# A hybrid SSM and attention decoder step on one core: SSM loads moved to ScalarE's queue, and probabilities scaled on VectorE

## The chip, the core and the metric

The kernel runs on one core of a Trainium2 chip. The core has five engines with a queue of instructions each: TensorE (PE, matrix products), VectorE (DVE), ScalarE (ACT), GpSimd (POOL) and SyncE (SP, used here for transfers only). The metric is the device time of one execution in microseconds. Three executions of the kernel before took 1873.18, 1874.78 and 1879.98 us; their median is 1874.78.

## The reference, cut to what matters

One layer of a decoder for 256 prompt positions and 8 x 4 sample positions, width 2048: a half-weighted SwiGLU block, a mixer, and a second SwiGLU block. All is float32. The mixer:

```python
z = rmsnorm(x) @ w_in                      # columns: u (1024), q (1024), k (256), v (256)
# SSM group: 64 groups of 16 channels, 64 complex states each
bu = einsum('blgc,gpc->blgp', u, B_bar)
h  = associative_scan(a = lam_bar, bu)      # h[t] = lam_bar * h[t-1] + bu[t]
y  = Re(einsum('blgp,gcp->blgc', h, C)) + D * u
y  = gelu(y);  y = y * sigmoid(y @ w_glu)   # 16x16 per group
# attention group: window 128, 16 query heads on 4 key heads, per-head sink
p  = exp(logits - m);  p = p / (p.sum() + exp(sink - m));  o = p @ v
x  = x + w_out @ concat(rmsnorm(y), rmsnorm(o))
```

The final SSM states, keys and values are outputs too.

## The kernel before

**Tokens and products.** All 288 tokens stand side by side as columns, 4 phases of 72 (8 sample columns and 64 chunks of 4 prompt positions). A float32 product is made as three: weight and activation are split into a high and a low part (`wh`, `wl`, `xh`, `xl`), and `mm3` (L286) issues high x high, low x high and high x low. One weight piece of 128 x 1024 feeds 24 such products of 288 columns.

**Slots.** The order of the whole kernel is written out by hand in class `Weights`. Each call of `next` (L138) is one slot: it splits the piece that is needed two slots later (a cast on ScalarE, L124, into one of 3 buffers, and a subtraction on VectorE, L125), issues the load of the piece six slots ahead on SP's queue (L116, 6 buffers), runs the functions that were put down for this slot (`at`, `spread`), and returns the piece, with which the caller issues its 24 products. So the small products of a slot stand ahead of its 24, and everything that a slot puts on an engine's queue is done in the order of the list. `spread` runs a generator up to its next `yield` in each slot; with `last=True` it starts behind all else in its slot.

**The mixer** begins at slot `base` = 304: 20 projections of two slots each (one key block, eight SSM blocks j = 0 to 7, one key block, two value blocks, eight query blocks), then 32 slots of the output projection. SSM block j is projected in slots base + 2j + 2 and + 3. Its further steps hang on s = base + 2j + 5:

- `ssm_u_store` (L760, slot s): the projected block goes to DRAM, on ScalarE's queue.
- `ssm_u_load` (L763, slot s + 2): four transfers bring it back with positions on other partitions, as tile `U`, on SP's queue.
- `ssm_load_a`, `ssm_load_r`, `ssm_load_b` (L769, L773, L787): tables `ma`, `rot` and `mb` of this block, written to DRAM during the first SwiGLU block, on SP's queue. `ma` and `mb` have two buffers each, `rot` three.
- `ssm_state` (L791, from slot s + 4): 32 small products of `ma` and `U` (L798, the state products), a rotation on VectorE, the scan (L814), a slot later the rotation back (L820 on POOL, L821) into `cs`, a slot later two corrections (L823, L824) and the copy of the final state on ScalarE (L825).
- `ssm_out` (L827, slot s + 9): 48 small products (L833, the output products) and a Gelu on ScalarE.
- `ssm_y_store`, `ssm_y_load` (L839, L845) for two blocks together: to DRAM in four transfers on ScalarE's queue, and back on SP's.
- `ssm_glu` (L853): one product (L856), Tanh, and `y_split`, which makes the high and low parts and adds the squares for the norm. `ssm_norm` (L898) turns the sum into a factor.

`put` is ScalarE's queue for transfers and `get` is SP's (L697).

**Attention.** For a pair of heads i: `q_square`, `sums` (L1017: row sums on TensorE; `row_rsqrt`, twelve small steps on POOL), `scores` (L1035: products, eviction on ScalarE with the factor from `row_rsqrt` (L1049), distance term on VectorE), `softmax` (L980: maximum on VectorE, Exp on ScalarE, sum and reciprocal on VectorE, the scaling on POOL, L1001), `probs_t` (L1056: transposes on TensorE, L1062) and `pv`. `sample` (L1089) does the same for the sample positions. All PSUM results go through eight tiles of one name (`main`), used in turn.

Of the kernel before, what the change touches and what calls it, by code (L numbers as in the profile page):

```python
# [14 lines left out]
ALU = mybir.AluOpType  # L15
AX = mybir.AxisListType

P = 128
# [15 lines left out]
EPS = 1e-6  # L34
# [656 lines left out]
def mix(tc, nc, io, es, W, base, e):  # L691
    act, dve, pool_e, pe = nc.scalar, nc.vector, nc.gpsimd, nc.tensor
    tt, ts, stt = dve.tensor_tensor, dve.tensor_scalar, dve.scalar_tensor_tensor
    x, R, gains, ident, acc = e["x"], e["R"], e["gains"], e["ident"], e["acc"]
    tp, dr, pm, pa = (e[k] for k in ("tp", "dr", "pm", "pa"))
    proj, mm3 = e["proj"], e["mm3"]
    put, get = act.dma_start, nc.sync.dma_start  # L697
# [7 lines left out]
    def aux():  # L705
        return pa.tile([P, 512], F32, name="main")
# [7 lines left out]
    R_ssm = mp.tile([P, N], F32, name="R_ssm")  # L714
# [7 lines left out]
    yd = [dr.tile([2 * P, N], F32, name="yd%d" % j) for j in range(4)]  # L722
# [8 lines left out]
    def y_split(pool, src, g, first, eng=pool_e):  # L731
        hh = pool.tile([P, N], F32R, name="hh", bufs=8)
        if first:
            pool.tile([P, 32], F32, name="gap_y", bufs=1)
        hl = pool.tile([P, N], F32R, name="hl", bufs=8)
        gc = gains[:, g:g + 1]
        act.activation(halved(hh), evens(src), AF.Copy, scale=gc)
        YH.append(hh)
        YL.append(hl)
        sq = tp.tile([P, N], F32, name="sq", bufs=3)  # L740
        act.activation(sq, src, AF.Square)
        yield
        stt(halved(hl), evens(src), gc, halved(hh.bitcast(F32)), op0=ALU.mult, op1=ALU.subtract)  # L743
        if first:
            eng.tensor_copy(acc, sq)
        else:
            eng.tensor_tensor(acc, acc, sq, op=ALU.add)


    MA, MB, ROT, D0, U, CS, UE, YG, YN, GL = ({} for _ in range(10))  # L750
    c4 = [P, 4, NCH]

    def flat(ap):
        return ap.rearrange("p q k -> p (q k)")
# [8 lines left out]
    def ssm_u_load(j):  # L763
        U[j] = sm.tile([P, 4, W1], F32, name="U", bufs=4)
        src = ud[j].rearrange("(q c) (j t) -> j c q t", q=4, j=T)
        for jr in range(T):
            get(U[j][32 * jr:32 * jr + 32], src[jr])

    def ssm_load_a(j):  # L769
        MA[j] = sa.tile([P, 2, 4, P], F32, name="ma", bufs=2)  # L770
# [20 lines left out]
    def ssm_state(j):  # L791
        ma, u, rot = MA.pop(j), U[j], ROT.pop(j)
        b = []
        for i in range(2):
            ps = aux()
            for q in range(4):
                for hh in HALVES:
                    pe.matmul(ps[hh, q * W1:(q + 1) * W1], ma[:, i, q, hh], u[:, q], start=True, stop=True)  # L798
            b.append(ps[:, :N].rearrange("p (q t) -> p q t", q=4))
        br, bi = b[0][:, :, NB:], b[1][:, :, NB:]  # L800
        co, si = rot[:, :, 0, :], rot[:, :, 1, :]
        z, w = (sa.tile([P, 2, 4, NCH], F32, name="r" + n, bufs=2) for n in "zw")
        q = slice(4 * j, 4 * j + 4)
        tt(z[:, 1], br, co, op=ALU.mult)
        tt(w[:, 1], bi, si, op=ALU.mult)
        tt(z[:, 0], bi, co, op=ALU.mult)
        tt(w[:, 0], br, si, op=ALU.mult)
        yield
        for i in range(2):
            tt(fin_s[:, i, q, :], b[i][:, :, :NB], fin_s[:, i, q, :], op=ALU.add)  # L810
        tt(z[:, 1], z[:, 1], w[:, 1], op=ALU.add)
        tt(z[:, 0], z[:, 0], w[:, 0], op=ALU.subtract)
        for i in range(2):
            dve.tensor_tensor_scan(flat(w[:, i]), flat(D0[j % 2]), flat(z[:, i]), 0.0, op0=ALU.mult, op1=ALU.add)  # L814
        yield
        cs = CS[j % 2]
        for i in range(2):
            act.copy(cs[:, i, :, :NB], e["h0"][:, 1 - i, q, :])
        both = [P, 2, 4, NCH]
        pool_e.tensor_tensor(z, w, si[:, None].to_broadcast(both), op=ALU.mult)  # L820
        tt(cs[:, :, :, NB + 1:], w, co[:, None].to_broadcast(both), op=ALU.mult)  # L821
        yield
        tt(cs[:, 1, :, NB + 1:], cs[:, 1, :, NB + 1:], z[:, 0], op=ALU.subtract)  # L823
        tt(cs[:, 0, :, NB + 1:], cs[:, 0, :, NB + 1:], z[:, 1], op=ALU.add)  # L824
        act.copy(fin[:, :, q], cs[:, :, :, W1])  # L825

    def ssm_out(j):  # L827
# [16 lines left out]

    def ssm_y_load(j):  # L845
        YN[j] = sm.tile([P, 2, N], F32, name="yn", bufs=2)
        get(YN[j], yd[j].rearrange("(a p) n -> p a n", a=2))

    def glu_load():
        GL[0] = sm.tile([P, 8, P], F32, name="gl")  # L850
# [2 lines left out]
    def ssm_glu(j):  # L853
        yn = YN[j // 2][:, j % 2]
        ps = aux()
        pe.matmul(ps[:, :N], GL[0][:, j], yn, start=True, stop=True)  # L856
        t = tp.tile([P, N], F32, name="s1")
        act.activation(t, ps[:, :N], AF.Tanh, scale=0.5)
        yield
        y2 = tp.tile([P, N], F32, name="s2")  # L860
        stt(y2, t, 1.0, yn, op0=ALU.add, op1=ALU.mult)
        yield
        yield from y_split(ys, y2, 48 + j, j == 0, dve if j == 7 else pool_e)
# [16 lines left out]
    for j in range(8):  # L880
        s = base + 2 * j + 5
        W.at(s, ssm_u_store, j)
        W.at(s + 1 if j > 1 else base + 1 + j, ssm_load_a, j)
        W.at(s + 1 if j > 1 else base + 2 + j, ssm_load_r, j)
        W.at(s + 2, ssm_u_load, j)
        W.at(s + 2, ssm_decay, j)
        W.spread(s + 4, ssm_state(j), True)
        W.at(s + 6, ssm_load_b, j)
        W.at(s + 9, ssm_out, j)
        if j % 2:  # L890
            W.at(s + 10, ssm_y_store, j // 2)
            W.at(s + 11, ssm_y_load, j // 2)
            W.spread(s + 13, ssm_glu(j - 1))
            W.spread(s + 14, ssm_glu(j))
    W.at(s + 8, state_done)
    W.at(s + 17, ssm_done)

    def ssm_norm():  # L898
        for n, _ in enumerate(e["norm"](e["ones"], acc, R_ssm, 1.0 / 1024, 4 * EPS)):
            if n % 2:  # L900
                yield

    W.spread(s + 19, ssm_norm())

    def tok(ap, blk):

# [73 lines left out]
    def softmax(lg, parts, sink, w):  # L980

        m = mp.tile([P, w], F32, name="sm_m", bufs=4)
        es_ = mp.tile([P, w], F32, name="sm_e", bufs=4)
        l = mp.tile([P, w], F32, name="sm_l", bufs=4)
        for a, (lo, hi) in enumerate(parts):
            dve.tensor_reduce(m[:, 2 * a:2 * a + 2], lg[:, :, lo:hi], axis=AX.X, op=ALU.max)
        tt(m, m, sink, op=ALU.max)
        tt(es_, sink, m, op=ALU.subtract)
        ts(m, m, -1.0, None, op0=ALU.mult)
        yield  # L990
        for a, (lo, hi) in enumerate(parts):
            for hb in range(2):
                c = 2 * a + hb
                act.activation(lg[:, hb, lo:hi], lg[:, hb, lo:hi], AF.Exp, bias=m[:, c:c + 1],  # L994
                               accum_out=l[:, c:c + 1])
        act.activation(es_, es_, AF.Exp)
        yield
        tt(l, l, es_, op=ALU.add)
        dve.reciprocal(l, l)
        for a, (lo, hi) in enumerate(parts):  # L1000
            pool_e.tensor_tensor(lg[:, :, lo:hi], lg[:, :, lo:hi],  # L1001
                                 l[:, 2 * a:2 * a + 2, None].to_broadcast([P, 2, hi - lo]), op=ALU.mult)

    def q_square(i):
        qb = QN[i]
# [29 lines left out]
    def scores(i):  # L1035
        p, g = divmod(i, 4)
        qb, sq = QN.pop(i)
        rq = RQ[i // 2][:, 4 * (i % 2):4 * (i % 2) + 4]
        pss = [aux() for _ in range(2)]
        for a, (bq, bk) in enumerate(((0, 0), (1, 0), (1, 1))):  # L1040
            for hb in range(2):
                pp = slice(64 * hb, 64 * hb + 64)
                pe.matmul(pss[hb][:, 128 * a:128 * a + 128], qb[pp, 128 * bq:128 * bq + 128],
                          tok(kG[pp, p], bk), start=True, stop=True)
        yield
        lg = L[i] = late["a"].tile([P, 2, 384], F32, name="lg", bufs=3)
        for hb in range(2):
            for blk, (lo, hi) in enumerate(((0, 128), (128, 384))):
                act.activation(lg[:, hb, lo:hi], pss[hb][:, lo:hi], AF.Copy,  # L1049
                               scale=rq[:, 2 * blk + hb:2 * blk + hb + 1])  # L1050
        yield
        for hb in range(2):
            stt(lg[:, hb], dist, -SLOPES[heads_of(i)[hb]], lg[:, hb], op0=ALU.mult, op1=ALU.add)
        yield from softmax(lg, ((0, 128), (128, 384)), sinkp[:, 4 * i:4 * i + 4], 4)
# [105 lines left out]
    for p in range(2):  # L1160
        s = base + 2 * (12 + 4 * p + 3) + 2
# [3 lines left out]
    for i in range(8):  # L1165
        p, g = divmod(i, 4)
# [186 lines left out]
```

## Time and profile before

| | before |
|---|---|
| median of 3 executions | 1874.78 us |
| profiled execution | 1878.1 us, span of its instructions 1876.2 us |
| TensorE clock granted, mean | 0.996 |
| VectorE, ScalarE, POOL busy | 64%, 45%, 14% of the span |
| DMA | 359.08 MB moved, 191 GB/s over the span |
| two SwiGLU blocks and w_in, w_out: large products | 14400 of 288 columns |

In the profile, "idle before, releaser" names what ended a wait by the semaphores seen in the trace; where the engine named had long been done, it was another, often a transfer. PEld is the weight load of TensorE, which runs beside its products. A "q" behind an engine's name (SPq, ACTq) is its queue of instructions, with the issue of transfers. The chain that ended last gives TensorE 93% of the span. In a list of transfers the last number is the median time from issue to landing.

### The profile page before, as it was taken

Reading aid. Unit: us, or ns where it says so; the run is one execution under the profiler, and the core shown is the slowest. Engines: PE = TensorE matmul, PEld = TensorE weight load, DVE = VectorE, ACT = ScalarE, POOL = GpSimd, SP = SyncE. Lnnn points to the kernel's source line nnn. Section 1 sums busy time; section 2 is a strip of 40 time slices with the busy share of each in tenths; the row PEclk is TensorE's granted clock in tenths of the full one; section 3 lists DMA queues with packets and bytes.
Section 4 is the critical chain, followed back from the end, with each engine's and each line's share of the span. In section 5 each row is a group of like instructions: output and inputs, shape, how many; then the busy total and the mean of one; then the engine's idle time right before and its main releaser. Section 6 shows DMA issues by size and latency. Waiting matters only on the chain.

```text
span 1876.2 us, 38183 instructions
## 1 busy us (share of the span) xinstructions
PE 1857.0 (99%) x15620; PEld 1839.1 (98%) x15620; DVE 1207.7 (64%) x1857; ACT 853.6 (45%) x1347; POOL 269.0 (14%) x342
## 2 busy tenths in 40 slices
PE   9999999999999999999989999999999999999999
PEld 9999999999999999998988999999999999999999
DVE  6677667666667755688887885555555555555554
ACT  6443444444444444643566554433444334434433
POOL 3201011000100100212236640000000000000000
PEclk9999999999999999999999999999999999999999
DMA  7555656556655764788733455556555565556555
GB/s 277 197 181 163 219 181 214 190 166 230 212 192 162 232 213 147 238 293 292 232 120 135 157 176 185 179 161 188 187 179 168 174 196 180 163 169 207 180 161 160
DMA packets 122624, 359.08 MB, mean 191 GB/s; under 512 B 22064, under 2 KB 30256, under 8 KB 121264
## 3 DMA queue, kind: packets, MB, share of 16 engines
q1 hardware_dynamic: 114496, 340.48, 56.7%
q10 hardware_dynamic: 7952, 16.16, 2.5%
q8 instruction: 122, 2.00, 0.4%
q14 instruction: 54, 0.44, 0.1%
HBM read 338.40 MB, written 20.22 MB: 191 GB/s over the span
## 4 chain that ended last, share of the span: by engine, by line
PE 93%; DVE 3%; ACT 1%; DMA 1%; POOL 1%; issue 1%; SPq 0%; ACTq 0%; POOLq 0%; DVEq 0%
PE main L290 30%; PE main L292 30%; PE main L291 30%; DVE wl L125 1%; ACT wh L124 1%; PE main L833 1%; DMA ud<-t 0%; PE main L798 0%; PE main L623 0%; PE main L629 0%; ACT lg L994 0%; DMA ma<-mats 0%; DMA raw<-in_w_gu 0%; POOL x L1178 0%; POOL lg L1001 0%
## 5 line engine op out<-in xcount | busy, mean ns | idle before, releaser
L125 DVE TENSOR_TENSOR wl<-raw,wh 128x1024 fp32r<-128x1024 f32 (+2 forms) x677 | 754.1, 1114 | 445.0 <-ACT wh L124 443.1
L290 PE MATMUL main<-xh,wh 128*128 128x288 f32 x3136 | 904.9, 289 | 0.5 <-ACT xh L216 0.5
L292 PE MATMUL main<-xh,wl 128*128 128x288 f32 x3136 | 899.7, 287 | 0.7 <-DVE wl L125 0.6
L291 PE MATMUL main<-xl,wh 128*128 128x288 f32 x3136 | 899.4, 287 | 0.1
L124 ACT CAST wh<-raw 128x1024 fp32r<-128x1024 f32 (+2 forms) x677 | 637.9, 944 | 495.9 <-PE main L291 335.4
L290 PEld LDWEIGHTS main<-xh,wh 128*128 128x128 f32 x3136 | 594.6, 190 | 3.9 <-ACT xh L216 0.8
L292 PEld LDWEIGHTS main<-xh,wl 128*128 128x128 f32 x3136 | 594.5, 190 | 1.7 <-DVE wl L125 0.8
L291 PEld LDWEIGHTS main<-xl,wh 128*128 128x128 f32 x3136 | 594.7, 190 | 1.3 <-DVE xl L217 0.8
L290 PE MATMUL main<-hh,wh 128*128 128x288 f32 x1664 | 478.2, 287 | 0.3 <-ACT s L1079 0.3
L291 PE MATMUL main<-hl,wh 128*128 128x288 f32 x1664 | 476.3, 286 | 0.6 <-DVE hl L743 0.6
L292 PE MATMUL main<-hh,wl 128*128 128x288 f32 x1664 | 476.2, 286 | 0.0
L290 PEld LDWEIGHTS main<-hh,wh 128*128 128x128 f32 x1664 | 314.8, 189 | 1.2 <-ACT s L1079 0.8
L291 PEld LDWEIGHTS main<-hl,wh 128*128 128x128 f32 x1664 | 314.8, 189 | 1.0 <-DVE hl L743 0.8
L292 PEld LDWEIGHTS main<-hh,wl 128*128 128x128 f32 x1664 | 314.8, 189 | 0.2 <-DVE wl L125 0.2
L364 POOL TENSOR_TENSOR s<-s,R 128x288 f32<-128x288 f32 x88 | 70.6, 803 | 1139.5 <-ACT s L363 1139.5
L373 ACT CAST hh<-h 128x288 fp32r<-128x288 f32 x88 | 38.1, 433 | 222.5 <-DVE h L372 222.5
L363 ACT ACTIVATE s<-t 128x288 f32<-128x288 f32 x88 | 39.1, 445 | 219.5 <-DVE t L362 219.5
L394 DVE SCALAR_TENSOR_TENSOR x<-main,x 128x288 f32<-128x288 f32 x128 | 58.4, 457 | 39.7 <-PE main L292 39.3
L372 DVE TENSOR_TENSOR h<-main,s 128x288 f32<-128x288 f32 x88 | 40.1, 456 | 55.5 <-PE main L292 55.2
L362 DVE TENSOR_TENSOR t<-main,R 128x288 f32<-128x288 f32 x88 | 40.2, 456 | 44.9 <-PE main L292 44.6
L374 DVE TENSOR_TENSOR hl<-h,hh 128x288 fp32r<-128x288 f32 x88 | 40.4, 459 | 44.0 <-ACT hh L373 44.0
L226 POOL TENSOR_TENSOR acc<-acc,sq 128x288 f32<-128x288 f32 x45 | 45.3, 1006 | 46.0 <-ACT sq L222 45.1
(262 smaller groups left out, 835.8 us busy)
## 6 DMA issues: line engine op xcount, KB each, us to landing
raw<-in_w_gu SPq DMA_DIRECT2D x349, 512.0 KB, 4.1
raw<-in_w_dn SPq DMA_DIRECT2D x128, 384.0 KB, 3.2
raw<-in_w_dn SPq DMA_DIRECT2D x128, 320.0 KB, 3.2
raw<-in_w_in SPq DMA_DIRECT2D x40, 512.0 KB, 4.9
raw<-in_w_out SPq DMA_DIRECT2D x32, 512.0 KB, 3.5
mats<-stage ACTq DMA_DIRECT2D x8, 1536.0 KB, 7.1
mb<-mats SPq DMA_DIRECT2D x8, 768.0 KB, 8.2
ma<-mats SPq DMA_DIRECT2D x8, 512.0 KB, 5.4
```

The lines of the kernel that those rows point to most:

```text
L124: self.nc.scalar.copy(wh[:, :n], t[:, :n])
L125: self.nc.vector.tensor_tensor(wl[:, :n], t[:, :n], wh[:, :n].bitcast(F32), op=ALU.subtract)
L226: eng.tensor_tensor(acc, acc, sq, op=ALU.add)
L290: pe.matmul(ps, wh[:, s], woven(rh[k]), start=first and a == 0, stop=False)
L291: pe.matmul(ps, wh[:, s], woven(rl[k]), start=False, stop=False)
L292: pe.matmul(ps, wl[:, s], woven(rh[k]), start=False, stop=last and a == n - 1)
L362: dve.tensor_tensor(t1, pg[:, :N], R, op=ALU.mult)
L363: act.activation(s1, t1, AF.Silu)
L364: pool_e.tensor_tensor(s2, s1, R, op=ALU.mult)
L372: dve.tensor_tensor(halved(h), evens(pu[:, :N]), evens(s2), op=ALU.mult)
L374: dve.tensor_tensor(hl, h, hh.bitcast(F32), op=ALU.subtract)
L394: dve.scalar_tensor_tensor(x[d], ps[:, :N], 0.5, x[d], op0=ALU.mult, op1=ALU.add)
```

## The change

The loads of `U` and of the SSM results go to ScalarE's queue. `U` is loaded one slot earlier; for j > 1 the tables `ma` and `rot` are loaded one slot earlier and the state products start one slot earlier and so fall into the slot of the output products of block j - 3. The copy of the final state runs one slot later. The second GLU block of a pair runs in the slot of the first. The norm of the SSM group starts one slot earlier and takes one step a slot. In `softmax`, the scaling moves from POOL (one instruction for two heads) to VectorE (one for each head, `ts` is `tensor_scalar`).

```diff
     def ssm_u_load(j):
...
         for jr in range(T):
-            get(U[j][32 * jr:32 * jr + 32], src[jr])
+            put(U[j][32 * jr:32 * jr + 32], src[jr])
...
         tt(cs[:, 0, :, NB + 1:], cs[:, 0, :, NB + 1:], z[:, 1], op=ALU.add)
+        yield
         act.copy(fin[:, :, q], cs[:, :, :, W1])
...
     def ssm_y_load(j):
         YN[j] = sm.tile([P, 2, N], F32, name="yn", bufs=2)
-        get(YN[j], yd[j].rearrange("(a p) n -> p a n", a=2))
+        put(YN[j], yd[j].rearrange("(a p) n -> p a n", a=2))
...
         W.at(s, ssm_u_store, j)
-        W.at(s + 1 if j > 1 else base + 1 + j, ssm_load_a, j)
-        W.at(s + 1 if j > 1 else base + 2 + j, ssm_load_r, j)
-        W.at(s + 2, ssm_u_load, j)
+        W.at(s + 1, ssm_u_load, j)
+        W.at(s if j > 1 else base + 1 + j, ssm_load_a, j)
+        W.at(s if j > 1 else base + 2 + j, ssm_load_r, j)
         W.at(s + 2, ssm_decay, j)
-        W.spread(s + 4, ssm_state(j), True)
+        W.spread(s + (3 if j > 1 else 4), ssm_state(j), True)
...
             W.spread(s + 13, ssm_glu(j - 1))
-            W.spread(s + 14, ssm_glu(j))
+            W.spread(s + 13, ssm_glu(j))
...
-    def ssm_norm():
-        for n, _ in enumerate(e["norm"](e["ones"], acc, R_ssm, 1.0 / 1024, 4 * EPS)):
-            if n % 2:
-                yield
-
-    W.spread(s + 19, ssm_norm())
+    W.spread(s + 18, e["norm"](e["ones"], acc, R_ssm, 1.0 / 1024, 4 * EPS))
...
         for a, (lo, hi) in enumerate(parts):
-            pool_e.tensor_tensor(lg[:, :, lo:hi], lg[:, :, lo:hi],
-                                 l[:, 2 * a:2 * a + 2, None].to_broadcast([P, 2, hi - lo]), op=ALU.mult)
+            for hb in range(2):
+                ts(lg[:, hb, lo:hi], lg[:, hb, lo:hi], l[:, 2 * a + hb:2 * a + hb + 1], None, op0=ALU.mult)
```

## The prediction, made before the result was known

> **What bounds the kernel now.** I read the page, then the waits of TensorE in the stretch of the mixer, then that stretch by windows, then the queues and engines around each wait.
>
> ```profile
> span 1876.2 us, 38183 instructions
> ...
> PE 1857.0 (99%) x15620; PEld 1839.1 (98%) x15620; DVE 1207.7 (64%) x1857; ACT 853.6 (45%) x1347; POOL 269.0 (14%) x342
> ```
>
> TensorE has work 99% of the time, so only its gaps and its slow stretches can be won. By stage:
>
> ```profile
> 843.40:900.00 56.60, 50.58 (x685) 47.50 (x685) 49.32 (x96) 22.08 (x47) 12.26 (x7) 0.97 0.82 271
> ...
> 940.00:1031.00 91.00, 84.86 (x808) 77.26 (x806) 71.32 (x151) 64.16 (x187) 48.18 (x74) 0.94 0.37 124
> ```
>
> The columns are the window, PE, PEld, DVE, ACT and POOL busy, granted clock, DMA share and GB/s. PE lacks 6.0 us in the SSM stage (843 to 900) and 6.1 in the attention stage (940 to 1031), and both run below full clock. The waits of PE in these two stretches:
>
> ```profile
> PE main L798 <- DMA U<-ud: 2.7, 1, 2.7
> PE main L798 <- ACT cs L818: 2.0, 1, 2.0
> PE main L798 <- DVE rw L814: 1.4, 1, 1.4
> ```
>
> ```profile
> PE main L1062 <- POOL lg L1001: 3.7, 3, 2.2
> PE main L1025 <- ACT qsq L1007: 2.1, 1, 2.1
> ```
>
> The state products (L798) wait three times, 6.1 us. Only the first is named as the load of U; in the others the engine named had long been done and the last U loads were still under way, so I count all three as late U. The transposes (L1062) wait for the scaling on POOL, and the sums (L1025) once.
>
> ```profile
> 873.00:876.40 3.40, 1.44 (x36) 1.25 (x34) 3.37 (x5) 1.78 (x4) 1.86 (x1) 1.00 0.74 213
> 876.40:879.80 3.40, 3.40 (x20) 3.26 (x16) 2.24 (x5) 0.00 (x0) 0.36 (x1) 0.50 1.05 400
> ...
> 951.40:958.30 6.90, 6.23 (x38) 4.73 (x39) 4.20 (x5) 5.42 (x14) 4.96 (x7) 0.51 0.50 176
> ...
> 985.60:989.00 3.40, 3.05 (x15) 2.50 (x13) 3.26 (x9) 3.40 (x14) 1.00 (x1) 0.50 0.48 154
> ```
>
> A stretch of 3.4 us in which PE was busy for 1.44 is followed by one at half clock; two more half-clock stretches lie in the attention stage, behind its longest waits. Such a stretch of 3.4 us, full of products, loses at most 3.4 x 0.5 = 1.7 us; I take 1.4, since part of it is small products and waiting. So a wait near 2 us costs up to 3.4. [...]
>
> **The U loads.** Why was U late?
>
> ```profile
> 854.08 8.37 SPq L767 DMA_DIRECT2D U<-ud  x4
> ```
>
> ```profile
> SPq L767 <- DMA ud<-t: 9.5, 3, 6.5
> SPq L767 <- DMA yd<-yg: 8.2, 1, 8.2
> ```
>
> SP sat 8.4 us on four U loads, with the weights and matrices of the next slots queued behind. It waited for the store of u (9.5 us in all), and 8.2 us for a store of y whose data U doesn't need: a transfer also waits until an earlier one with its semaphore has landed. Then everything SP held back goes out together and the next U loads lie behind it. After the change SP issues only raw, ma, rot and mb, and the U loads go out on ScalarE one slot earlier, while the products that use them come one slot earlier too for j > 1. So I set the time from store to use against two landings. The lengths:
>
> ```profile
> 836.19 1.15 PE main L798 x32
> 843.42 1.15 PE main L798 x32
> 847.71 1.68 PE main L833 x48
> ```
>
> From 836.19 to 843.42 lie 1.15 us of state products and two slots: 3.04 us a slot. From j = 3 on, the slot of the state products is also that of output products: 3.04 + 1.68 + 1.15 = 5.87; a pair of slots is 8.9. The store of u goes out, I take it, 0.5 us into its slot, behind the wait of one cast, and the state products can start 3.04 + 5.87 + 3.04 + 1.68 = 13.6 us after that slot began. Four issues of U take 1.9 us (0.43 each in the first row below, and about 0.05 between them). That leaves 13.6 - 0.5 - 1.9 = 11.2 us for both landings.
>
> ```profile
> L767 SPq DMA_DIRECT2D U<-ud x32: 302/428/1456, 822.9 to 895.9; - x32
> ...
> DMA to landing us min/median/max: 1.8/5.7/8.5
> ```
>
> ```profile
> U<-ud SPq DMA_DIRECT2D x20, 36.0 KB, 7.5
> ud<-t ACTq DMA_DIRECT2D x4, 144.0 KB, 5.1
> yd<-yg ACTq DMA_DIRECT2D x8, 72.0 KB, 5.7
> ```
>
> The last three are of 843 to 900. The store takes 5.1. No row has U on ScalarE's queue; the bounds are the 1.8 and the 8.5 of all 32 loads. I take 5.7, from the y stores, packets of the same 288 B on ScalarE's queue. 5.1 + 5.7 = 10.8 fits into 11.2, barely; I leave 1.0 us in sum for five groups. For j = 2 the gap is shorter, because no output products run yet. The same list for 826 to 843:
>
> ```profile
> U<-ud SPq DMA_DIRECT2D x9, 36.0 KB, 5.2
> ud<-t ACTq DMA_DIRECT2D x2, 144.0 KB, 4.6
> ```
>
> On ScalarE the four loads of j = 0 stand ahead of the store of j = 1: from 822.9 (where SP starts them today, on the landing of their data) to 824.8. The store lands at 829.4; the loads of j = 1 run to 831.3; the store of j = 2 leaves near 831.7 and lands at 836.3; its last load leaves at 837.8 and lands at 843.0. The products want it at 836.19 + 1.15 + 3.04 = 840.4, one slot before today's 843.42. A wait of 2.6 (none with 1.8, 5.9 with 8.5), plus half of a half-clock stretch, 0.7. SSM stage: 2.6 + 0.7 + 1.0 = 4.3 us where 6.1 + 1.4 = 7.5 stand now: **3.2 us won**.
>
> Behind the U loads on ScalarE stand the casts (L124), then VectorE's subtract (L125) and PE. The cast held until 831.3 and its subtract (1.23 below, the cast about as long) are done near 833.7; the slot that needs them begins its products after 836.19 + 1.15 = 837.3. So I cost it at nothing; the cover is 3.6 us, used up if a store took 8.2 to land. The y load waits on ScalarE for its four stores; only y pair 0 meets U loads (j = 6), and GLU needs it two slots on: nothing.
>
> **The final states.**
>
> ```profile
> L825 ACT COPY fin<-cs 128x8 f32<-128x8 f32 x8 | 1.6, 206 | 16.4 <-DVE cs L824 16.4
> ```
>
> The copy one slot later removes 16.4 us of waiting on ScalarE, 2 us a group. PE doesn't wait for it now; it is the room that the four issues need (1.9). Zero by itself. Both GLU blocks in one slot put four ScalarE steps where two were, and the norm begins a slot earlier in single steps; both lie under PE's 3.04 us of products a slot, with two slots of casts as cover: zero, within 0.5 either way.
>
> **The probabilities.** The multiplies leave POOL for VectorE.
>
> ```profile
> L460 DVE TENSOR_SCALAR rtm<-rf 128x256 f32<-128x256 f32 x16 | 4.6, 290 | 0.3
> ...
> L460 DVE TENSOR_SCALAR p<-p 128x160 f32<-128x160 f32 x2 | 0.5, 239 | 0.0
> ```
>
> Two of 256 columns at 0.29 and two of 128 at about 0.24 make 1.06 us for each of 8 score tiles, 0.48 for each sample: 9.4 us more on VectorE, some 1.1 a slot. Where it counts:
>
> ```profile
> 946.70 0.18 DVE L999 RECIPROCAL sm_l<-sm_l 128x4 f32<-128x4 f32 x1
> ...
> 947.81 1.23 DVE L125 TENSOR_TENSOR wl<-raw,wh 128x1024 fp32r<-128x1024 f32 x1 [0.51 <-ACT wh L124]
> ```
>
> ```profile
> 946.72 0.21 POOL L974 TENSOR_TENSOR rq_t<-rq_t,rq_v 128x10 f32<-128x10 f32 x1
> ...
> 947.88 1.22 POOL L974 TENSOR_TENSOR rq_t<-rq_t,rq_v 128x10 f32<-128x10 f32 x1
> ...
> 950.88 1.61 POOL L1001 TENSOR_TENSOR lg<-lg,sm_l 128x256 f32<-128x256 f32 x2
> ```
>
> ```profile
> 951.55 0.48 PE L1062 MATMUL main<-ident,lg 128*128 128x128 f32 x1 [2.17 <-POOL lg L1001]
> ...
> 953.80 0.64 PE L1100 MATMUL main<-kG,qs 64*128 64x32 f32 x4
> ```
>
> ```profile
> 950.96 1.36 ACT L1049 ACTIVATE lg<-main,rq_o 128x128 f32<-128x128 f32 x4 [2.86 <-POOL rq_o L976]
> ```
>
> The divisor is there at 946.9, but POOL first works through the chain of rq and scales only at 950.9. VectorE would have scaled by 948.0, before the transposes are due (951.55 - 2.17 = 949.4). What is late next: the sample's scores (L1100) in the same slot take the PSUM tile that ScalarE empties with L1049, after rq_o, not before 951.7. So L1100 starts its second half near 951.8 instead of following at 953.8: 2.0 to 2.5 us won, not 4.7. I take 2.5, and 0.4 for the shorter half-clock stretch. A rule against the edit: the small POOL step at 947.88 took 1.22 beside VectorE's two-input subtract, against 0.21 for its like. [...]
>
> The sums' wait (2.1) hangs on VectorE, which works through six steps of the norm in that slot:
>
> ```profile
> 977.04 1.18 DVE L235 TENSOR_TENSOR rt<-rt,rv 128x288 f32<-128x288 f32 x1
> ...
> 979.24 0.46 DVE L235 TENSOR_TENSOR rt<-rt,rv 128x288 f32<-128x288 f32 x1
> ```
>
> Single steps of the norm take three of these out of the slot, 3 x 0.46 = 1.4, and without POOL's scaling beside it a step like the first is 0.7 shorter; the scaling adds 0.5 to 1.1. 1.4 us won, and half of the half-clock stretch, 0.7. The third wait of L1062 goes too, 3.7 - 2.17 - 0.5 (right behind the first) = 1.0. In sum 2.5 + 0.4 + 1.4 + 0.7 + 1.0 = **6.0 us**, between 2.4 (1.4 + 1.0, had the chain of rq waited its full 1.06 and the sums gained nothing) and 8.6 (both waits, 5.8, and two half-clock stretches).
>
> Together 9.2 us off the profiled execution's 1878.1 (span 1876.2). The median of the three runs is 3.3 lower, and I take the difference off it: 1874.8 - 9.2 = **1865.6**.
>
> **Rivals.** (1) All waits named go, with their half-clock stretches: 7.5 + 5.8 + 1.4 x 2 = 16.1, so 1858.7. For it: U leaves a slot earlier and SP's hold-ups end; against it L1049 and j = 2 above. (2) The queue changes nothing in the landing: U stays at 7.5. Then 5.1 + 7.5 = 12.6 is 1.4 over; a wait in one group gives time to the next, so half of it counts, 0.7 x 5 = 3.5; j = 2 waits 837.8 + 7.5 - 840.4 = 4.9; two half-clock stretches 2.8: 11.2, a loss of 3.7, against 6.0 won: 1872.5. For it speaks that U was behind other transfers, not behind its own queue; against it the y stores' 5.7 beside U's 7.5. [...] (3) Slower: the path from store to load becomes the bound.
>
> ```profile
> 854.84 7.29 DMA ud<-t
> ```
>
> With the store at 7.3 and U at 8.5 the sum is 15.8, 4.6 over: 2.3 x 5 = 11.5, 5.9 for j = 2 and four half-clock stretches 5.6 make 23.0, 15.5 more than now, against 6.0: 1884.3. It decides above a sum of about 13 us. The DMA share of 0.82 speaks for it, SP's freed queue against.
>
> **Numbers.** Forecast 0.50 (its own range 1860 to 1871), rival 1 0.25, rival 2 0.18, rival 3 0.07. 0.5% is 9.4 us, about what a measurement of this kernel can tell from no change, and puts the lines at 1865.4 and 1884.2. The forecast's half falls evenly to either side of the first. Faster 0.25 + 0.25 = 0.50, same 0.25 + 0.18 = 0.43, slower 0.07. Range 1856 to 1877: without rival 3 and the outer edges of 1 and 2.
>
> **What would show it.** Right: no wait of L1062 for the scaling, a wait at L1100 near 2 us, the U loads on ACTq landing near 5.7, one wait of L798 near 2.6 us early (j = 2) and under 1 us in sum later, clock above 0.97 in 843 to 900. Wrong: casts on ScalarE waiting for ud, U landing above 7, or PE waiting for L125.

## The result, and the profile after

The changed kernel takes 1887.39 us (median of four runs, 1886.21 to 1888.46); four runs of the kernel before have the median 1874.49 (1873.18 to 1879.98). The ratio of the two kernels is 1.0055, 95% interval 1.004 to 1.0069; the two medians alone divide to 1.0069, its upper edge. That is slower by 0.5%, where 0.5% faster was forecast, and outside the range. The profiled execution took 1886.8 us, 8.7 more than that of before. Its line numbers are one higher than before from L826 on (the GLU product is L857, the load of y L848) and five lower in the attention (the sums L1020, the transposes L1057, the sample's scores L1095).

The page's totals for the changed kernel:

```profile
span 1885.0 us, 38195 instructions
...
PE 1859.1 (99%) x15620; PEld 1841.7 (98%) x15620; DVE 1207.5 (64%) x1893; ACT 850.7 (45%) x1347; POOL 243.8 (13%) x324
```

VectorE's busy time hardly changed although it took over the scaling, POOL's fell by 25 us, and the span grew by 8.8. The stages by windows (columns as in the prediction), first of the changed kernel, then the three windows of the kernel before that were not shown yet:

```profile
826.00:843.40 17.40, 13.69 (x154) 12.98 (x152) 15.15 (x30) 6.16 (x10) 2.37 (x3) 1.00 0.84 279
843.40:900.00 56.60, 50.61 (x679) 47.73 (x680) 43.74 (x94) 17.84 (x38) 6.87 (x6) 0.94 0.89 283
900.00:925.00 25.00, 23.97 (x254) 22.74 (x254) 20.78 (x41) 11.81 (x29) 4.54 (x7) 1.00 0.64 192
925.00:940.00 15.00, 12.24 (x122) 11.43 (x121) 6.73 (x11) 3.82 (x9) 4.85 (x14) 0.77 0.70 225
940.00:1031.00 91.00, 85.82 (x806) 79.33 (x807) 73.75 (x190) 67.39 (x197) 25.21 (x53) 0.96 0.37 121
```

```profile
826.00:843.40 17.40, 17.40 (x187) 16.81 (x185) 17.16 (x31) 6.27 (x9) 3.26 (x3) 1.00 0.93 313
900.00:925.00 25.00, 25.00 (x298) 23.48 (x296) 22.50 (x43) 11.35 (x26) 6.50 (x7) 1.00 0.84 289
925.00:940.00 15.00, 15.00 (x140) 14.30 (x139) 9.00 (x20) 9.36 (x21) 4.17 (x14) 1.00 0.57 176
```

PE lacked nothing in these three windows before; now it lacks 3.7, 1.0 and 2.8 us there, as much as before in the SSM stage (6.0) and 1.0 less in the attention stage (5.2 for 6.1). That is 18.7 us in sum for 12.2, 6.5 more. The rest is clock: 0.94 for 0.97 in the SSM stage, 0.77 for 1.00 at 925 to 940, 0.96 for 0.94 in the attention. Weighted by the windows, 56.6 x 0.03 + 15 x 0.23 - 91 x 0.02 = 3.3 us. 6.5 + 3.3 = 9.8, near the 8.8 by which the span grew. So the attention stage won about 2.8 us, and everything ahead of it lost about 12.6.

What PE waited for in 800 to 1120 of the changed kernel:

```profile
PE main L798 <- DMA U<-ud: 3.8, 2, 3.5
PE main L857 <- DMA yn<-yd: 3.6, 2, 2.6
PE main L798 <- DMA rot<-mats: 3.4, 1, 3.4
PE main L1020 <- ACT qsq L1002: 2.8, 1, 2.8
PE main L1095 <- ACT lg L1044: 2.4, 2, 2.2
```

The third of these waits is one for U as well: the state products (L798) do not read `rot`, and they started at 866.12, about when the last load of U for j = 4, issued at 856.3, landed (the loads of this block took 8.4 to 10.0 us). Two of the waits were not foreseen at all: the GLU product waits for y (L857), and the sums wait for ScalarE's squares (L1020) 50 us earlier than they did. ScalarE's own timeline shows why for the second:

```profile
925.53 0.45 ACTq L923 DMA_DIRECT2D out_kT<-s  x1
...
926.98 0.40 ACT L859 ACTIVATE s<-main 128x288 f32<-128x288 f32 x1
932.15 0.41 ACT L859 ACTIVATE s<-main 128x288 f32<-128x288 f32 x1 [4.77 <-DMA out_kT<-s]
...
932.75 0.42 ACT L1002 ACTIVATE qsq<-qn 128x256 f32<-128x256 f32 x1
```

The two tanh steps (L859) of the third pair (j = 4 and 5) stand in one slot. The second takes the buffer that the store of kT still reads, and holds ScalarE for 4.8 us, with the squares that PE needs behind it.

### The profile page after: what moved, and what is told of

Same layout as the page of the kernel before. It is cut to its first block, busy times and chain, and to the rows that moved or that the text cites. A ratio compares the mean times of both kernels' runs of the same rounds, so it can differ in the third digit from the quotient of the medians.

```text
span 1885.0 us, 38195 instructions
## 1 busy us (share of the span) xinstructions
PE 1859.1 (99%) x15620; PEld 1841.7 (98%) x15620; DVE 1207.5 (64%) x1893; ACT 850.7 (45%) x1347; POOL 243.8 (13%) x324
## 4 chain that ended last, share of the span: by engine, by line
PE 90%; DVE 3%; DMA 3%; ACT 2%; issue 1%; POOL 1%; ACTq 0%; DVEq 0%; POOLq 0%; SPq 0%
PE main L290 29%; PE main L292 29%; PE main L291 29%; DVE wl L125 1%; DMA U<-ud 1%; DMA ud<-t 1%; ACT wh L124 1%; PE main L623 0%; PE main L629 0%; DMA out_kT<-s 0%; DMA raw<-in_w_in 0%; POOL x L1173 0%; ACTq L767 0%; DVE sm_m L981 0%; PE main L1057 0%
## 5 line engine op out<-in xcount | busy, mean ns | idle before, releaser
L125 DVE TENSOR_TENSOR wl<-raw,wh 128x1024 fp32r<-128x1024 f32 (+2 forms) x677 | 756.2, 1117 | 462.8 <-ACT wh L124 460.8
L1173 POOL TENSOR_TENSOR x<-x,t 128x288 f32<-128x288 f32 x32 | 47.8, 1497 | 51.8 <-DVE t L1172 51.1
```

What stands on the lines that cost most here:

```text
L125: self.nc.vector.tensor_tensor(wl[:, :n], t[:, :n], wh[:, :n].bitcast(F32), op=ALU.subtract)
L1173: eng.tensor_tensor(x[d], x[d], t, op=ALU.add)
```

## The experiments

My theory at first: three separate losses, the y load on ScalarE, both GLU blocks in one slot, and the state products that come early for U. The rival: one delay of the chain from store to load, all of it from the queue of U. Each ratio below is against the kernel before, run beside it on the same chip; the interval behind it holds 95%, and a thousandth is 1.9 us.

**The scaling alone**, in the kernel before:

```diff
-            pool_e.tensor_tensor(lg[:, :, lo:hi], lg[:, :, lo:hi], ...
+            for hb in range(2):
+                ts(lg[:, hb, lo:hi], lg[:, hb, lo:hi], l[:, 2 * a + hb:2 * a + hb + 1], None, op0=ALU.mult)
```

> The kernel before with only the scaling of the probabilities moved from POOL to VectorE. In the profile of the whole change the attention stage (940 to 1031 us) is idle on PE for 5.2 us in place of 6.1, at a clock of 0.96 in place of 0.94 (91 x 0.02 = 1.8). Theory A, the scaling itself makes this gain: 1874.5 - 2.7 = 1871.8, with the transposes' waits gone and one of about 2.4 us at the sample's scores. Theory B, the prediction's price without the norm's steps (2.5 + 0.4 + 1.0 = 3.9): 1870.6. Theory C, the wait only changes its place, and the gain of the whole change there is due to its norm in single steps: 1874.5.

0.998 (0.9969 to 0.999), 3.7 us faster. PE's waits in the attention of this kernel:

```profile
PE main L1025 <- ACT qsq L1007: 2.3, 1, 2.3
PE main L1100 <- ACT lg L1049: 2.0, 1, 2.0
```

The transposes no longer wait for POOL, and 2.0 us come back at the sample's scores. Theories A (2.7) and B (3.9) both lie inside the interval, C (0) doesn't.

**The whole change with one edit taken back**, three times:

```diff
-            W.spread(s + 13, ssm_glu(j))
+            W.spread(s + 14, ssm_glu(j))
```

> The whole change, with the second GLU block of a pair back one slot later. Theory A: in the whole change the tanh of the second block waited 4.8 us on ScalarE for the store of kT, whose buffer it takes; the squares behind it came late, PE waited 2.96 us and then ran two windows at half clock (about 3.1 us lost). One slot later the store has landed: 1887.4 - 6.1 = 1881.3. Theory B: the stores that leave together at 924 to 926 hold ScalarE whatever the order of the GLU blocks, and the y stores wait on the same transfers: 1887, with the wait at 930 in place.

1.0054 (1.0041 to 1.0067): no gain. But the wait at 930 is gone (PE is busy for 15.00 us of 925 to 940). In its place stands

```profile
PE main L242 <- DVE acc L747: 2.9, 1, 2.9
```

and half-clock stretches behind it (granted clock 0.92 at 940 to 1031, 0.96 in the changed kernel): the norm, which the change starts one slot earlier, now waits for the last block of GLU. Each theory had half of it.

```diff
-        put(YN[j], yd[j].rearrange("(a p) n -> p a n", a=2))
+        get(YN[j], yd[j].rearrange("(a p) n -> p a n", a=2))
```

> The whole change, with the load of y back on SyncE's queue. Theory A: on ScalarE the load stands behind the four y stores and the copies and casts; PE waited for y 2.86 and 1.32 us, with about 2 us at half clock behind the first: with the load on SP 1887.4 - 5.9 = 1881.5. Theory B: the load waits for the landing of the stores wherever it is issued, and on SP it holds the weights up (8.2 us in the kernel before): no change or a loss, 1887 to 1890.

1.0031 (1.0019 to 1.0043), 4.5 us of the 10.3 back. PE no longer waits for y, but for U more than before:

```profile
PE main L798 <- DMA U<-ud: 5.5, 4, 3.8
PE main L798 <- DMA rot<-mats: 3.6, 1, 3.6
```

```diff
-            put(U[j][32 * jr:32 * jr + 32], src[jr])
+            get(U[j][32 * jr:32 * jr + 32], src[jr])
```

> The whole change, with the four loads of U back on SyncE's queue, still one slot earlier than before. Theory A, the queue is what costs: the waits of the state products, 3.75 and 3.58 us with 1.7 at half clock, go and 1887.4 - 9.0 = 1878.4. Theory B, the products that come one slot earlier are what costs, and the landing is the same from either queue: the waits stay and SP's wait for the store of u holds back weights and matrices besides: 1887 to 1892.

1.0022 (1.0013 to 1.0032), 6.2 us back. The waits of the state products go, as theory A said, though they come one slot early as before; the wait for y grows:

```profile
PE main L857 <- DMA yn<-yd: 4.3, 2, 2.6
...
PE main L798 <- DMA U<-ud: 0.6, 1, 0.6
```

**Both loads back on SyncE** (the last two edits together):

> The whole change with both loads, of U and of y, back on SyncE's queue. With U alone there the ratio to the kernel before fell from 1.0055 to 1.0022, with y alone to 1.0031. Theory A, each queue move costs by itself, because ScalarE stands at the issue until the store has landed: 3.3 + 2.4 thousandths together, 1.0055 - 0.0057 = 0.9998, and no wait of PE for U or y above 1 us. Theory B, they are one and the same delay of a chain, which the one or the other removes: no better than U alone, 1.0022.

1.0006 (0.9997 to 1.0015). The two queue moves cost 4.9 thousandths, 9.2 us, of the change's 5.5. The gains of the single edits (2.4 and 3.3) nearly add up, which speaks for theory A; but its sign, no wait above 1 us, fails: PE still waits 3.2 us for y once, with the load on SyncE.

**GLU block and norm back**, both loads left on ScalarE:

```diff
-            W.spread(s + 13, ssm_glu(j))
+            W.spread(s + 14, ssm_glu(j))
...
-    W.spread(s + 18, e["norm"](e["ones"], acc, R_ssm, 1.0 / 1024, 4 * EPS))
+    W.spread(s + 19, ssm_norm())
```

> The whole change, with the second GLU block one slot later and the norm of the SSM as it was (its steps two at a time, from one slot later on). With the GLU block alone put back the wait at 930 us and its half clock went, but PE waited 2.9 us for the norm's sum of squares and lost 3.2 in the half-clock windows behind it, and nothing was gained. Theory A, both edits together cost the 6.1 us at 930, and apart each hides the other: ratio 1.0055 - 6.1 / 1875 = 1.0022. Theory B, something else takes the place again, as in that run: 1.005.

1.0026 (1.0013 to 1.0039), 2.9 thousandths better: theory A. The two edits hide each other. With the norm alone put back:

> The whole change with the norm of the SSM alone put back to its old slot and its steps two at a time. With the GLU block alone put back the ratio stayed at 1.0054, with both back it was 1.0026. Theory A, the GLU blocks in one slot cost by themselves (the tanh waits for the store of kT at 930 us, and PE behind it), and the early norm costs only where the GLU block is late: 1.0055, the wait of about 3 us at 930 in place. Theory B, the early norm is what costs: 1.003.

1.0071 (1.0056 to 1.0085), theory A again: the bunched GLU blocks cost by themselves. Whether the early norm saves something beside them (1.0055 with it) lies inside the intervals.

**What is left of the change**: both loads on SyncE, GLU and norm as before; U read one slot after its store, matrices and state products one slot earlier, the final states later, the scaling on VectorE.

> What is left of the change: U read one slot after its store, the matrices and the state products one slot earlier, the final states copied a slot later, the probabilities on VectorE; both loads on SyncE's queue, GLU and norm as before. Theory A, the losses add up: the change costs 1.0055, of which 5.7 thousandths are the two queues and 3.3 the GLU block with the norm: 0.9965, 6.6 us below the kernel before, which beats the scaling alone (0.998). Theory B, the earlier state products cost as much as the earlier loads win: 0.998, as the scaling alone.

0.9981 (0.9971 to 0.999), the same as the scaling alone. So GLU and norm cost 2.5 thousandths here too (1.0006 - 0.9981), but the early products and loads give nothing: theory B. The waits for U that were to be won are in fact won, and y is late in their place:

```profile
PE main L857 <- DMA yn<-yd: 3.3, 1, 3.3
...
PE main L798 <- DMA U<-ud: 0.7, 1, 0.7
```

**The GLU blocks of the first pair one slot later**, to take that wait away:

```diff
-            W.spread(s + 13, ssm_glu(j - 1))
-            W.spread(s + 14, ssm_glu(j))
+            W.spread(s + (14 if j == 1 else 13), ssm_glu(j - 1))
+            W.spread(s + (15 if j == 1 else 14), ssm_glu(j))
```

> Both loads on SyncE, GLU and norm as before, U and state products early (the run with the ratio 0.9981), and the GLU blocks of the first pair one slot later. Theory A: there the waits for U were gone (0.7 us in sum), but PE then waited 3.3 us for y of the first pair, 0.6 more and about 1.7 at half clock behind it; one slot later y is there: 0.9981 - 5.6 / 1875 = 0.9951, the best so far. Theory B: the time is taken again by the next wait, and the early products give nothing: 0.998.

0.9985 (0.9977 to 0.9994), not better. Now y is there, and U is late again:

```profile
PE main L798 <- DMA U<-ud: 3.0, 1, 3.0
...
PE main L857 <- DMA yn<-yd: 0.7, 1, 0.7
```

With the norm in single steps as well:

> As the run with the GLU blocks of the first pair one slot later, and the norm in single steps from its old slot on. Theory A, the gains add: 2.1 us less than that run, 0.9951 - 0.0011 = 0.994. Theory B, the norm's single steps only move the wait: as that run.

0.9979 (0.9966 to 0.9991): within the interval of the scaling alone. No version of mine beats that one measurably.

**The scaling and the norm in single steps**, in the kernel before:

```diff
-    W.spread(s + 19, ssm_norm())
+    W.spread(s + 19, e["norm"](e["ones"], acc, R_ssm, 1.0 / 1024, 4 * EPS))
```

> The kernel before with the scaling on VectorE and the norm of the SSM in single steps, begun in its old slot. Theory A, the prediction's step: the sums' wait of 2.1 to 2.3 us hangs on VectorE's six steps of the norm in that slot; single steps take 1.4 off it and half a half-clock stretch, 0.7: 2.1 us beside the scaling's 0.998, so 0.9969. Theory B, the squares are late for another reason, or the wait moves to the next product: 0.998, as the scaling alone.

0.9985 (0.9977 to 0.9994): nothing beside the scaling, theory B. The sums' wait is gone, and the transposes (L1056 in this kernel) wait for ScalarE instead:

```profile
PE main L1056 <- ACT s L1073: 1.7, 1, 1.7
...
PE main L1056 <- ACT lg L1043: 0.8, 1, 0.8
```

**The state products back at their old place**, both loads on ScalarE and the rest of the change kept, but for the copy of the final states, which is as before:

```diff
-        W.spread(s + (3 if j > 1 else 4), ssm_state(j), True)
+        W.spread(s + 4, ssm_state(j), True)
```

> The whole change, but the state products at their old place, two slots behind the matrices and three behind the loads of U, and the final states copied as before; both loads stay on ScalarE. Theory A, the early products are what makes the queue's delay dear: the waits for U of 3.75 and 3.58 us go, 1.0055 - 7.3 / 1875 = 1.0016. Theory B, ScalarE held at the issues is what costs, since the stores and casts behind it are late too: the products wait again or the y products do, 1.004 to 1.005.

1.0056 (1.0044 to 1.0068): theory B, no gain at all. U isn't late any more, and y is, by as much and more:

```profile
PE main L856 <- DMA yn<-yd: 8.8, 2, 6.1
...
PE main L798 <- DMA U<-ud: 1.0, 3, 0.3
```

**The queues alone, in the kernel before.** Whether the queue as such costs, or the engine that stands at the issue, was still open. Five runs take it apart; their edits are `put` for `get` at U, at y, or at both, and U at `s + 1` for `s + 2`. U on ScalarE at its old place:

> The kernel before with one edit: the four loads of U on ScalarE's queue, at their old place two slots behind the store. Theory A, the queue costs because the issue holds ScalarE while the store of u is under way; two slots later the store has nearly landed, so it costs little: 0.999 to 1.002, ScalarE's casts waiting less than 3 us in sum for ud. Theory B, the queue itself costs, wherever the loads stand: U lands later and the products wait, as in the whole change, ratio 1.003 to 1.004.

1.0014 (1.0005 to 1.0022), in the range of theory A. The same, one slot earlier:

> The kernel before with the four loads of U on ScalarE's queue and one slot earlier; the products stay where they were. Two slots behind the store the same edit had the ratio 1.0014. Theory A, what costs is that ScalarE stands at the issue until the store of u has landed, with stores of y, casts and copies behind it: 1.004 or more, with PE waiting for y or for late u. Theory B, the queue as such costs, and an earlier issue can only help: 1.0014 or less.

1.001 (1.0 to 1.002). Theory A falls: ScalarE standing at the issue of U costs no more than a later issue. One slot earlier on SyncE:

> The kernel before with the four loads of U one slot earlier on SyncE's queue, where nothing computes. Theory A (the held engine is what costs): no loss, 0.999 to 1.0005, the waits for U shorter than before and something else late in their place. Theory B, the blind prediction's sum for the loads: the waits of 6.1 us and 1.4 at half clock fall by 3.2 or more, 0.998 or less.

1.0001 (0.9993 to 1.0009). Nothing lost and nothing gained; in its profile PE waits 2.0 us for U, and 3.9 for y, which it didn't before:

```profile
PE main L856 <- DMA yn<-yd: 3.9, 1, 3.9
...
PE main L798 <- DMA U<-ud: 2.0, 1, 2.0
```

The load of y alone on ScalarE:

> The kernel before with the load of y alone on ScalarE's queue. Theory A, it costs what it cost in the changed kernel, 1.6 (with U on SyncE) to 2.4 thousandths (with U on ScalarE): 1.0016 to 1.0024, with PE waiting for y. Theory C, y is late only because the changed kernel comes to it earlier: 1.0005 or less.

1.0026 (1.0015 to 1.0036), 4.9 us: theory A by the time, but not by its sign. In the profile of this run the load of y leaves at 874.18, no later than before (874.12), and PE waits only 1.1 us for it. PE lacks 4.7 us at 843 to 900 (6.0 before) and 7.5 at 940 to 1031 (6.1 before). The profiled execution, at 1877.68 us, was the fastest of the twelve (median 1880.10), so how the 4.9 us come about is not shown. Both, with U early:

> The kernel before with both loads on ScalarE's queue, U one slot earlier, all else as it was. Theory A, the two loads make the loss by themselves, because they hold each other's engine (the y load waits for the y stores, behind which the next u store and U loads stand): 1.0045, as both queues cost in the changed kernel. Theory B, they add up from what each costs alone (1.0 for U, 1.6 to 2.4 for y): 1.0026 to 1.0034. Theory C, the rest of the change makes them dear: 1.001 to 1.002.

1.0054 (1.004 to 1.0069). The two queue edits alone lose what the whole change loses: theory A. The sum of the single edits, 1.0 + 2.6 = 3.6, lies just below the interval, that with the other run of U (1.4 + 2.6) at its edge; that the two together cost more than their sum is likely, not shown. And with the matrices one slot earlier:

> As e20, and the matrices of j > 1 loaded one slot earlier, as in the change. Theory A or B, the matrices don't matter: as e20. Theory C, 1 MB of matrices ahead of the U loads in the same slot is what delays them on the shared transfer engines: 1.5 thousandths or more above e20.

1.0056 (1.0041 to 1.0071): no more than without them, within the intervals.

What happens is seen on ScalarE with both loads on its queue, and nothing else changed but U's slot:

```profile
858.68 0.34 ACTq L761 DMA_DIRECT2D ud<-t  x1
...
860.26 0.40 ACT L837 ACTIVATE yg<-main 128x288 f32<-128x288 f32 x1
865.56 2.40 ACTq L767 DMA_DIRECT2D U<-ud  x4
868.01 0.21 ACT L825 COPY fin<-cs 128x8 f32<-128x8 f32 x1 [7.35 <-issue]
...
868.17 7.27 ACTq L843 DMA_DIRECT2D yd<-yg  x4
875.48 0.40 ACT L785 COPY d<-e 128x252 f32<-128x252 f32 x1 [6.32 <-DMA yd<-yg]
...
881.37 0.39 ACTq L847 DMA_DIRECT2D yn<-yd  x1
```

```profile
886.44 1.32 PE L856 MATMUL main<-yn,gl 128*128 128x288 f32 x2 [7.18 <-DMA yn<-yd]
```

and in the kernel before, ScalarE's y stores and SP's load of y:

```profile
861.61 5.89 ACTq L843 DMA_DIRECT2D yd<-yg  x4
```

```profile
874.12 0.38 SPq L847 DMA_DIRECT2D yn<-yd  x1
```

Read the first of these fences from top to bottom: it is one line of transfers, each of which needs an earlier one to have landed. The chain that ended last, taken for 855 to 890 of this run, goes the same way, from the store of u to the load of y:

```profile
858.68 6.81 DMA ud<-t
...
866.44 8.16 DMA U<-ud
...
874.97 6.24 DMA yd<-yg
...
881.37 5.03 DMA yn<-yd
```

Its second link is not one of data: the y stores don't read U, and yet the last two left only when the U load of 866.44 had landed, at 874.6. The store of u goes out at 858.68, the U loads can't go before 865.56, and ScalarE does nothing from 860.7 on. The y that it finished at 860.7 leaves behind them, at 868.17 instead of 861.61; the next copy waits 6.3 us, and the load of y goes out at 881.37 instead of 874.12. PE waits 7.18 us for it. Had it left at 874.12 and taken the same 5.03 us, it would have been there at 879.15, and PE came to the product at 879.26: the 7.25 us by which the load is late are this wait. Against the kernel before, where the product starts at 881.19, the loss is 5.3 us. With the loads on SP there were two lines: the first y store left at 861.61, ahead of the last of the U loads that SP began at 854.08 (862.14).

## Why the prediction was wrong, point by point

- **The y load** was the step that failed: "only y pair 0 meets U loads (j = 6), and GLU needs it two slots on: nothing". In the changed kernel PE waited 3.6 us for y in two places, and with this load back on SyncE's queue the wait is gone and 4.5 us are won. Alone, in the kernel before, the move costs 4.9 us (1.0026), of which that run's profile shows only 1.1 as a wait for y. With U's loads on ScalarE as well the wait is 7.5 us and the loss that of the whole change (1.0054). I followed what waits behind the loads on ScalarE as far as the casts, which had cover, and not to the y stores and the load of y behind these, which had none. The sum for "11.2 us for both landings" took the store's issue at 0.5 us into its slot as given; it too stands in that line.
- **The landing** was near the forecast in the middle, and too long in one group. The median from issue to landing was 6.6 us at 843 to 900, where 5.7 was forecast and 7.5 stood before. But the loads for j = 4 took 8.4 to 10.0, and the state products waited 3.4 us for them, where 1.0 was left for all five groups. With j = 2 they waited 7.2 us in sum, for 3.6 forecast and 6.1 before. The median of 826 to 905, before and after:

```profile
U<-ud SPq DMA_DIRECT2D x28, 36.0 KB, 6.3
```

```profile
U<-ud ACTq DMA_DIRECT2D x28, 36.0 KB, 6.1
```

  These two rows differ in the slot too. In the kernel before with only U's loads changed, the same median is 6.3 on SyncE's queue and 6.5 on ScalarE's two slots behind the store, and 4.2 and 6.3 one slot behind it (one execution each; in the changed kernel 4.3 and 6.1). Two slots behind the store the queue made a difference of 0.2 us, one slot behind it of 2.1. A cause that fits, not tested: SyncE, while it stands at the loads of U, sends no weights ahead of them (in the kernel before none left between 854.08 and 862.87).
- **The wait at j = 2** was right in mechanism and near in price: 2.6 forecast, 3.5 measured. ScalarE's timeline shows the store at 830.6 (forecast 831.7) and the loads from 835.6 to 838.5 (the last forecast to leave at 837.8):

```profile
830.62 0.34 ACTq L761 DMA_DIRECT2D ud<-t  x1
...
835.59 2.95 ACTq L767 DMA_DIRECT2D U<-ud  x4
...
839.17 1.05 ACT L124 CAST wh<-raw 128x1024 fp32r<-128x1024 f32 x1 [5.38 <-DMA U<-ud]
```

  The last row is close to the sign that the prediction itself named for being wrong: a cast held for 5.4 us, though behind the loads of U, which had waited for ud. No wait of PE for a cast stands in the list of its waits.
- **The 3.2 us of the SSM stage** failed even with the loads on SyncE. U's waits went (0.7 us left) and the time stayed: PE, earlier by that much, met the next transfer that wasn't there, y, and with y moved U again. I summed waits as if each could be taken out alone. The 6.1 us were also the most that U can have held: in the two waits not named as U, the engine named had not long been done but ended together with the wait (the copy at 875.2, the scan at 898.0). The two runs with these waits (ratios 0.9981 and 0.9985) had the DMA engines 83 to 94% busy at 826 to 925, and in each PE waited for the next transfer, 3.3 us for y in the one and 3.0 for U in the other. That the sum of the transfers is the bound there is argued, not shown.
- **Both GLU blocks in one slot and the early norm**, "zero, within 0.5 either way", cost 2.5 to 2.9 thousandths, 4.7 to 5.4 us. I counted ScalarE's steps and not whose buffer the second block takes: that of the kT store, then under way.
- **The final states**: zero forecast. No run tested it alone; with the early products and loads it gives zero.
- **The scaling** was right: 2.5 + 0.4 + 1.0 = 3.9 forecast, 3.7 measured (1.9 to 5.8 by the interval), with the wait of about 2 us at the sample's scores (2.0 in that run, 2.4 in the changed kernel). VectorE was busy for 4.1 us more in that run (1211.8 for 1207.7), where 9.4 were forecast. No run shows the 1.06 us by which the lower end of the range (1.4 for 2.5) lets the scalings hold the chain of rq: in the changed kernel POOL's steps beside them (1.01 us each from 958.66 and from 961.58) took 0.20 to 0.38 us, and the one that took 1.19, at 960.13, stood beside the subtract (L125).
- **The norm in single steps**, 2.1 us, failed: the sums' wait goes, and the transposes wait for ScalarE a slot earlier or later (1.7 and 0.8 us).

The sum of the runs: 5.4 thousandths for the queues, 2.5 for GLU and norm, -2.0 for the scaling, 0 for the rest: 5.9, where 5.5 was measured. Rival 3 had the right side and nearly the right size (1884.3) but mostly for another reason: it priced longer landings in every group (U at 8.5), and only j = 4 had them; the larger part of the loss is in transfers that started late and in the GLU blocks.

## What to carry to other kernels

Before a load moves to another queue, write down that queue's whole order of transfers with what each must wait for, and follow the line to the last transfer in it, not only to the engine's own work: here the U loads that waited for a store held the y stores and the y load behind them too, and a y store that left 6.6 us later (868.17 for 861.61) came out as 7.2 us of TensorE's waiting. Before two steps go into one slot, look at who still reads the buffers that they take (here the kT store, for 4.8 us). Where several waits lie close together in a stage that its transfers nearly fill (83 to 94% here), price the removal of one at nothing until the next late transfer has been named; here only the edit in the attention stage paid, where the DMA engines were busy for 37% of the time.

## What the runs showed of the hardware

In the changed kernel the clock falls to 0.50 at 844.2, 885.2, 933.0, 963.7 and 977.4 us, for 3.41 us each time and for twice that at 933.0. The wait of PE just before or around it ends at 843.5, 884.9, 933.2, 963.5 and 976.4, so the fall comes between 0.2 us ahead of that end and 1.0 behind it. The falls are 41.0, 47.8, 30.7 and 13.7 apart, which is 12, 14, 9 and 4 times 3.41. Of the two cases below, the longer wait is spread over two pieces of this raster and the shorter lies in one:

```profile
861.35:864.75 3.40, 1.41 (x46) 1.26 (x42) 3.37 (x9) 1.18 (x2) 1.06 (x1) 1.00 0.86 277
864.75:868.15 3.40, 2.04 (x39) 1.99 (x40) 3.09 (x6) 0.02 (x1) 0.20 (x1) 1.00 0.81 259
881.80:885.20 3.40, 0.83 (x5) 0.57 (x5) 0.00 (x0) 1.18 (x4) 0.00 (x0) 1.00 0.99 320
885.20:888.60 3.40, 3.40 (x34) 2.49 (x34) 3.12 (x8) 0.52 (x2) 0.00 (x0) 0.50 0.36 108
```

The wait of 3.4 us at 862 to 866 lies across two pieces, with PE busy for 1.41 and 2.04 us in them, and the clock stays at 1.00; the shorter one at 882 lies in one piece, 0.83 busy, and the next runs at 0.50. Behind pieces that were busy for 0.83 and, before, 1.44 us the clock fell, and behind one with 1.41 it didn't, so the busy time alone doesn't decide. Nor did a busy piece always end it: 933.0 to 936.4 was busy for 3.19 us at half clock, and the next piece ran at 0.50 too. So the raster is shown by the distances; by what a piece decides is not shown.
